# A transformer trunk layer: x loaded by features, W_ada packed for whole rows and cut into eleven groups, and the second runs of partial sums added last

## The chip, the cores and the metric

The kernel runs on one core of one Trainium2 chip. The metric is device time in microseconds (us), the median over runs of the kernel before; a single execution is also recorded by the hardware profiler, and all rows below come from that one. Engines: PE is TensorE (matmuls), DVE is VectorE, ACT is ScalarE, POOL is GpSimd, SP issues most transfers.

## The reference, cut to what matters

There are 512 tokens and 2048 features. One layer computes, in float32:

```python
mod = silu(c) @ W_ada + b_ada           # shift_a, scale_a, gate_a, shift_f, scale_f, gate_f
h = rms_norm(x) * (1 + scale_a) + shift_a
proj = h @ w_in                          # q/k/v, indexer q/k, latents, gates
y = W_o(sigmoid(g_a) * (o_A @ W_pA) + sigmoid(g_b) * (o_B @ W_pB))
x = x + gate_a * y
h = rms_norm(x) * (1 + scale_f) + shift_f
x = x + gate_f * (W_down(silu(conv(h W_up)_gate) * conv(h W_up)_value))
```

`o_A` is an attention over the keys that a top-k of indexer scores selects, `o_B` a dense causal attention. Only the part from `x` to a first share of the columns of `proj` is touched by the change.

## The kernel before

The 2048 features are 16 tiles of 128 (called tile 0 to 15). Each float32 factor is split into a high part `hi`, rounded by ACT, and a low part `lo`, the remainder, taken by DVE; a product is then three matmuls (hi·hi, hi·lo, lo·hi). For activations the split is L423 (ACT, hi) and L424 (DVE, lo), for weights L133 (ACT) and L134 (DVE).

**The first projection stage** computes the indexer's columns (name A, 1104 columns) and the keys, values and some gate columns (name B, 512 + 384 = 896 columns). Its unit is an *item*: one feature tile times one of the two column blocks, so A0 to A15 and B0 to B15, 32 items. An item is 21 matmuls of 128x512 (`quarter_k`) into seven of the eight PSUM banks. `PLAN` is a table that sets the order of items: all A items that follow one another without a B between them are one *run*, accumulated in the banks; as the last item of a run ends, `fin` stores the run's seven sums (`part`), or adds them to those of an earlier run on DVE (L376).

**The modulation** has to be there before an item: tile k of `h` needs scale and shift of tile k, which are 2 x 128 columns of `silu(c) @ W_ada`. Before, the 16 tiles are eight *groups* of two. For a group, 16 pieces of W_ada (one per 128 rows of the sum, each 128 rows x 2 x 256 columns, so two runs of 1 KB to a row) are loaded by SP (L328); DVE multiplies each by its entry of `silu(c)` and adds it up over the pieces (L339, L341; five of group 0's pieces go over PE instead, L333); PE sums over the partitions with a vector of ones (`ada_sum`, L347); DVE makes the columns (`ada_cols`, L312 and L354); and ACT applies scale and shift (L422) and rounds (L423).

**The start** loads x by tokens (4 x 4 tiles of 128x512), takes the squares with row sums on ACT (L268) and DVE (L266), the inverse root on POOL, scales rows (L274, L276), and turns x by 64 PE transposes of 128x128 (L297) with 16 copies by ACT (L301). Until the first item is ready, `keep_warm` (L254) puts small matmuls on PE.

**The order of the work.** Each engine has its own queue and takes it strictly in turn. The order in each queue is not the order of the source: a planner plays the program through with its own costs and decides; `tc.issue_after` and `tc.high_priority` bend it. Weights pass through five raw buffers and three pairs of hi/lo buffers, so that an item's split waits until the matmuls of the item three before it have ended. After the stage come the rotary tables (DVE), a transpose of the positions, further projections, and the indexer's scores (L598, L602), and much later the long stages of the FFN.

## Time and profile before

| | |
|---|---|
| time of the kernel, three runs | 2651.3, 2648.29, 2647.92 us; median 2648.29 us |
| span of the profiled execution | 2648.6 us, 0.3 us above the median |
| first matmul of the first projection stage | 37.95 us |
| end of its last matmul | 216.8 us |
| PE busy, whole span | 98% |

PE is busy nearly all of the time, so what the change can move lies in the first 8 per cent of the span. How to read a row: a group row has line, engine, operation, output<-input, shape and count, then busy time and mean ns of one, then the idle time of the engine just before these instructions and what ended it. A timeline row has start, duration and the instructions taken together, and in brackets the wait ahead of them with its releaser. A windows row has the stretch and its length, then the busy time of each engine, the clock that PE was granted (1.00 is full), and the share and rate of the transfers.

### The profile page before, as it was taken

Reading aid. Unit: us, or ns where it says so; the run is one execution under the profiler, and the core shown is the slowest. Engines: PE = TensorE matmul, PEld = TensorE weight load, DVE = VectorE, ACT = ScalarE, POOL = GpSimd, SP = SyncE. Lnnn points to the kernel's source line nnn. Section 1 sums busy time; section 2 is a strip of 40 time slices with the busy share of each in tenths; the row PEclk is TensorE's granted clock in tenths of the full one; section 3 lists DMA queues with packets and bytes.
Section 4 is the critical chain, followed back from the end, with each engine's and each line's share of the span. In section 5 each row is a group of like instructions: output and inputs, shape, how many; then the busy total and the mean of one; then the engine's idle time right before and its main releaser. Section 6 shows DMA issues by size and latency. Waiting matters only on the chain. (4 is left out here: it accounts for less than half of the span.)

```text
span 2648.6 us, 45089 instructions
## 1 busy us (share of the span) xinstructions
PE 2593.5 (98%) x17268; PEld 2349.6 (89%) x17268; DVE 2176.9 (82%) x3486; ACT 1249.7 (47%) x1951; POOL 366.0 (14%) x671
## 2 busy tenths in 40 slices
PE   8999999999999999999999999999999998999999
PEld 7777687779998777888789999999999998999999
DVE  7987975788878786975669899899899998878787
ACT  5333434344435544322545555555555556556454
POOL 1000011010022223200100000000000033314120
PEclk9999999999999999999999999999999999999999
DMA  9953135755675589974324433434434456767563
GB/s 342 344 163 100 36 100 188 228 155 169 198 243 178 156 273 352 301 254 137 135 74 145 145 115 130 144 116 130 145 124 140 148 173 190 206 163 214 141 198 114
DMA packets 215661, 464.32 MB, mean 175 GB/s; under 512 B 23786, under 2 KB 65156, under 8 KB 215444
## 3 DMA queue, kind: packets, MB, share of 16 engines
q1 hardware_dynamic: 170260, 344.93, 40.4%
q0 software_dynamic: 45152, 116.50, 14.9%
q8 instruction: 135, 2.21, 0.3%
q14 instruction: 82, 0.67, 0.1%
q10 hardware_dynamic: 32, 0.01, 0.0%
HBM read 397.11 MB, written 64.23 MB: 174 GB/s over the span
## 5 line engine op out<-in xcount | busy, mean ns | idle before, releaser
L1108 PE MATMUL bank<-slot,whl 128*128 128x256 f32 x3920 | 1103.0, 282 | 17.6 <-ACT slot L1008 5.9
L1109 PE MATMUL bank<-slot,whl 128*128 128x256 f32 x3920 | 1097.6, 281 | 0.7 <-DVE slot L142 0.7
L1110 PE MATMUL bank<-slot,whl 128*128 128x256 f32 x3920 | 1088.4, 282 | 6.1 <-DVE whl L142 6.1
L141 ACT ACTIVATE whl<-raw 128x1024 fp32r<-128x1024 f32 (+2 forms) x560 | 532.2, 953 | 632.6 <-PE bank L1109 408.7
L1108 PEld LDWEIGHTS bank<-slot,whl 128*128 128x128 f32 x3920 | 738.8, 189 | 24.5 <-ACT whl L141 7.9
L1109 PEld LDWEIGHTS bank<-slot,whl 128*128 128x128 f32 x3920 | 740.9, 189 | 1.1 <-DVE slot L142 0.9
L1110 PEld LDWEIGHTS bank<-slot,whl 128*128 128x128 f32 x3920 | 732.4, 188 | 7.2 <-DVE whl L142 7.1
L142 DVE TENSOR_TENSOR whl<-raw,whl 128x1024 fp32r<-128x1024 f32 (+2 forms) x560 | 605.6, 1087 | 131.9 <-ACT whl L141 123.7
L133 ACT ACTIVATE whl<-raw 128x1024 fp32r<-128x1024 f32 (+4 forms) x182 | 187.3, 1031 | 374.1 <-PE bank L147 184.3
L1004 DVE TENSOR_TENSOR raw<-raw 128x1024 f32<-128x1024 f32 (+2 forms) x320 | 347.4, 1086 | 4.9 <-DMA raw<-in_w_ups 1.4
L134 DVE TENSOR_TENSOR whl<-raw,whl 128x1024 fp32r<-128x1024 f32 (+4 forms) x182 | 215.8, 1186 | 154.7 <-ACT whl L133 148.3
L145 PE MATMUL bank<-whl,slot 128*128 128x512 f32 (+2 forms) x768 | 294.0, 395 | 9.3 <-ACT slot L423 6.1
L146 PE MATMUL bank<-whl,slot 128*128 128x512 f32 (+2 forms) x768 | 298.5, 389 | 0.4 <-DVE whl L134 0.4
L147 PE MATMUL bank<-whl,slot 128*128 128x512 f32 (+2 forms) x768 | 291.7, 385 | 0.0
L145 PE MATMUL bank<-slot,whl 128*128 128x512 f32 (+1 forms) x656 | 264.0, 406 | 6.1 <-DVE slot L733 3.8
L146 PE MATMUL bank<-slot,whl 128*128 128x512 f32 (+1 forms) x656 | 266.5, 407 | 1.9 <-DVE slot L741 1.9
L147 PE MATMUL bank<-slot,whl 128*128 128x512 f32 (+1 forms) x656 | 257.8, 401 | 0.1
L778 DVE SCALAR_TENSOR_TENSOR slot<-slot,c_act,slot 128x512 f32<-128x512 f32 x203 | 150.8, 748 | 45.4 <-DMA slot<-in_w_ada 43.5
L145 PEld LDWEIGHTS bank<-whl,slot 128*128 128x128 f32 x768 | 146.6, 192 | 41.7 <-ACT slot L423 6.8
L146 PEld LDWEIGHTS bank<-whl,slot 128*128 128x128 f32 x768 | 146.2, 190 | 30.2 <-issue 1.7
L147 PEld LDWEIGHTS bank<-whl,slot 128*128 128x128 f32 x768 | 144.7, 189 | 29.3 <-issue 0.7
L145 PEld LDWEIGHTS bank<-slot,whl 128*128 128x128 f32 (+1 forms) x656 | 123.8, 189 | 37.1 <-DVE slot L733 4.2
(292 smaller groups left out, 2722.2 us busy)
## 6 DMA issues: line engine op xcount, KB each, us to landing
slot<-in_w_ada SPq DMA_DIRECT2D x344, 256.0 KB, 5.3
raw<-in_w_ups SPq DMA_DIRECT2D x160, 512.0 KB, 3.6
raw<-in_w_in SPq DMA_DIRECT2D x50, 512.0 KB, 3.5
raw<-in_w_down SPq DMA_DIRECT2D x64, 384.0 KB, 4.8
raw<-in_w_down SPq DMA_DIRECT2D x64, 320.0 KB, 4.2
slot<-f POOLq DMA_DIRECT2D x154, 128.0 KB, 4.1
f<-slot POOLq DMA_DIRECT2D x66, 256.0 KB, 5.3
raw<-in_w_gs SPq DMA_DIRECT2D x32, 512.0 KB, 4.4
```

The lines of the kernel that those rows point to most:

```text
L133: A.activation(hi, raw[:, :w], AF.Copy)
L134: V.tensor_tensor(lo, raw[:, :w], r32(hi), ALU.subtract)
L141: A.activation(dst_hi, src, AF.Copy)
L142: V.tensor_tensor(dst_lo, src, r32(dst_hi), ALU.subtract)
L145: PE.matmul(o, lh, rh, start=first, stop=False)
L146: PE.matmul(o, lh, rl, start=False, stop=False)
L147: PE.matmul(o, ll, rh, start=False, stop=last)
L778: V.scalar_tensor_tensor(acc, ts[i], c_act[:, k:k + 1], acc, op0=ALU.mult, op1=ALU.add)
L1004: V.tensor_tensor(o[:, :W], a[:, :W], b[:, :W], op)
L1108: PE.matmul(o, wh[:, ks], rh, start=first and k == 0, stop=False, skip_group_check=True)
L1109: PE.matmul(o, wh[:, ks], rl, start=False, stop=False, skip_group_check=True)
L1110: PE.matmul(o, wl[:, ks], rh, start=False, stop=last, skip_group_check=True)
```

## The change

1. **x by features.** The host hands over x transposed as well, and L208 loads 16 tiles of 128 features x 512 tokens. ACT squares each (L271), DVE adds the squares (15 adds, L273), four small matmuls with ones sum over the partitions (L275), POOL takes the inverse root, PE spreads it over all partitions (L286) and DVE copies it out (L288, the tile `rbc`). Transposes and their copies are gone. Each tile of x is multiplied by `rbc` on DVE (`normed`, L302), two groups ahead of its use.
2. **W_ada packed.** The host packs the columns of shift and scale (`w_first`) so that each 128x512 piece has one run of 2 KB to a row (L329). A piece of a one-tile group holds two k pieces.
3. **Eleven groups**, `GROUPS`: tiles 0, 1, 2, 3 alone, then five pairs, then 14 and 15 alone. The first product of a group is ACT's (L348), others DVE's (L350, 256 or 512 wide), and some go over PE (L361): eight of group 0's, one of each of groups 4 to 8, two of the last two. A group's products are issued behind the columns (L374) of the group before it.
4. **The sum's place.** `SUM_IN` names the item inside which a group's sum stands in the source: B0 A1 A2 B3 B5 A7 A9 B11 A13 A14 for groups 1 to 10. It is the item, or the item but one, ahead of the first that needs the group.
5. **Order of items**: A0 B0 B1 A1 A2 A3 B2 to B7 A4 to A11 B8 to B13 A12 to A15 B14 B15.
6. **Runs.** The first and the second run of A and of B are stored by ACT (L416) in tiles of their own; third and, for B, fourth runs are added on DVE (L414) to the first. The fourteen adds of second into first (L396) are issued behind the last tile of h.
7. The keep-warm counts change to 42, 10 and 8, small constants on POOL move behind the inverse root, weights of four items are requested ahead, and the transpose of the positions (L521, L522) is issued behind the last tile of h.

The core of the diff, with what is only renamed left out:

```diff
+GROUPS = ((0, 1), (1, 1), (2, 1), (3, 1), (4, 2), (6, 2), (8, 2), (10, 2), (12, 2), (14, 1), (15, 1))
...
-    PLAN="A0 A1|A2 A3|B0 B1 B2 B3|A4 A5 A6 A7|B4 B5 B6 B7|A8 A9 A10 A11|B8 B9 B10 B11|A12 A13 A14 A15 B12 B13 B14 B15",
+    PLAN="A0 B0|B1 A1|A2|A3 B2 B3|B4 B5|B6 B7 A4 A5 A6 A7|A8 A9|A10 A11 B8 B9 B10 B11|B12 B13 A12 A13|A14|A15 B14 B15",
...
-    PEU=((2, 5, 8, 11, 14),) + ((),) * 7,
-    WU=(50, 20),
+    PEU=((0, 1, 4, 5, 8, 9, 12, 13),) + ((),) * 3 + ((15,),) * 5 + ((7, 15),) * 2,
+    SUM_IN='B0 A1 A2 B3 B5 A7 A9 B11 A13 A14',
+    WU=(42, 10, 8),
...
+        xs = [get() for _ in range(KD)]
+        for k in range(KD):
+            SP.dma_start(xs[k], xT_in[k * P:(k + 1) * P, :])
...
+    for k in range(KD):
+        t = sqx[(k - 1) % 5 + 1] if k else ssq
+        last_a = A.activation(t, xT[k], AF.Square)
+        if k:
+            V.tensor_tensor(ssq, ssq, t, ALU.add)
...
+    rbc = bcast_rows(rstd, bank[4])
+    last_h = [last_copy[0], last_a, last_copy[0]]
+
+    def normed(ks):
         for k in ks:
-            t = get()
-            A.activation(t, bank[k % 7], AF.Copy)
-            xT.append(t)
+            last_h[2] = V.tensor_tensor(xT[k], xT[k], rbc, ALU.mult)
...
+    def ada_mults(g):
         acc = accs[g % 2]
+        k0, n = GROUPS[g]
+        w = 2 * n * P
+        with tc.issue_after(last_h[2].ins):
...
+                    elif g not in begun:
+                        begun.add(g)
+                        with tc.issue_after(last_h[1].ins):
+                            A.activation(o, raw, AF.Copy, scale=c_act[:, k:k + 1])
+                    else:
+                        V.scalar_tensor_tensor(o, raw, c_act[:, k:k + 1], o, op0=ALU.mult, op1=ALU.add)
...
+    def next_tiles(g):
+        if g:
+            with tc.issue_after(mm_last[0].ins):
+                ada_sum(g)
+            mod_tiles(g)
+            if g + 2 < NG_A:
+                with tc.issue_after(last_h[2].ins):
+                    normed(range(GROUPS[g + 2][0], sum(GROUPS[g + 2])))
+            if g + 1 < NG_A:
+                ada_mults(g + 1)
             else:
...
+                        with tc.issue_after(last_h[0].ins):
+                            V.tensor_tensor(t[0:r], t[0:r], u[0:r], ALU.add)
+                        put(u)
...
+                t = part[name, min(runs[name], 3) % 3 or 1][i][0:r]
+                if runs[name] > 2:
                     V.tensor_tensor(t, t, b, ALU.add)
-                elif i % 2:
-                    V.tensor_copy(t, b)
                 else:
-                    A.activation(t, b, AF.Copy)
+                    last_h[1] = A.activation(t, b, AF.Copy)
...
-    V.tensor_copy(pos_f, posi)
+    with tc.issue_after(last_h[0].ins):
+        V.tensor_copy(pos_f, posi)
```

How the instructions stand in the queues shows at three places. **PE, a group's sum.** First PE's queue before, at the third sum, that of tiles 4 and 5, which item A4 is the first to need. `bank_73` is the bank of the modulation sums, `slot_351` the accumulated products; `slot_453` and `slot_454` are hi and lo of tile 1, `slot_516` the hi of tile 2.

```order
L147 MATMUL bank_70<-slot_453,whl 128x512
L147 MATMUL bank_71<-slot_453,whl 128x512
L147 MATMUL bank_72<-slot_453,whl 128x512
L347 MATMUL bank_73<-ones,slot_351 128x1 x4
L145 MATMUL bank_66<-whl,slot_516 128x512
L145 MATMUL bank_67<-whl,slot_516 128x512
L145 MATMUL bank_68<-whl,slot_516 128x512
```

Behind that sum stand B2 and B3, two items on tiles made long before. Now PE's queue of the changed kernel, at the sum of group 1 (tile 1): `slot_327` and `slot_328` are hi and lo of tile 0, `slot_445` the hi of tile 1.

```order
L155 MATMUL bank_71<-slot_327,whl 128x512
L153 MATMUL bank_72<-slot_327,whl 128x512
L154 MATMUL bank_72<-slot_328,whl 128x512
L155 MATMUL bank_72<-slot_327,whl 128x512
L361 MATMUL bank_73<-ones,slot_251 128x1 x2
L153 MATMUL bank_66<-whl,slot_445 128x512
L154 MATMUL bank_66<-whl,slot_445 128x512
L153 MATMUL bank_67<-whl,slot_445 128x512
```

Directly behind the sum stand the matmuls of item B1 on tile 1, whose hi is made from that very sum. The sums stand so, directly ahead of the item that needs them, at B0|B1, A1|A2, A2|A3, B3|B4, B5|B6, A9|A10, A13|A14 and A14|A15; inside A7 and B11 nine matmuls still follow the sum.

**DVE, the end of the stage.** First DVE's queue before, from the last lo of h (L424) on; `bank_66` and so on are the sums of the last run of A, `pos_c` the positions.

```order
L424 TENSOR_TENSOR slot_1350<-slot_354,slot_1349 128x512
L134 TENSOR_TENSOR whl<-raw,whl 128x1104 x2
L134 TENSOR_TENSOR whl<-raw,whl 128x896 x2
L376 TENSOR_TENSOR slot_406<-slot_406,bank_66 128x512
L376 TENSOR_TENSOR slot_409<-slot_409,bank_67 128x512
```

Then the changed kernel's DVE queue at the end of the adds of second runs; eleven more of them stand ahead of the first row, directly behind the last lo of h (L471).

```order
L396 TENSOR_TENSOR slot_519<-slot_519,slot_259 128x512
L396 TENSOR_TENSOR slot_524<-slot_524,slot_263 128x512
L396 TENSOR_TENSOR slot_529<-slot_529,slot_270 128x512
L136 TENSOR_TENSOR whl<-raw,whl 128x896 x2
L521 CAST slot_130<-slot_130 4x128
L414 TENSOR_TENSOR slot_393<-slot_393,bank_66 128x512
L414 TENSOR_TENSOR slot_398<-slot_398,bank_67 128x512
```

Between the last lo of h and the splits of the last two weights (L136, for B14 and B15) all fourteen adds of second runs have been put; the transpose of the positions (L522), which reads what L521 makes, stands on PE between A15 and B14.

**DVE, the first group.** The changed kernel's DVE queue from the copy of `rbc` (L288) to the first columns: the split of A0's weights (L136) stands ahead of the products of group 0, accumulated in `slot_250`.

```order
L288 COPY slot_241<-bank_70 128x512
L302 TENSOR_TENSOR slot_89<-slot_89,slot_241 128x512
L136 TENSOR_TENSOR whl<-raw,whl 128x1104
L350 SCALAR_TENSOR_TENSOR slot_250<-slot_255,c_act,slot_250 128x256
L350 SCALAR_TENSOR_TENSOR slot_250<-slot_259,c_act,slot_250 128x256 x2
L350 SCALAR_TENSOR_TENSOR slot_250<-slot_263,c_act,slot_250 128x256 x2
L350 SCALAR_TENSOR_TENSOR slot_250<-slot_270,c_act,slot_250 128x256 x2
L310 TENSOR_TENSOR mod<-bank_73,col_132 128x1 x2
L374 SCALAR_TENSOR_TENSOR s_a<-mod,col_132 128x1
```

DVE has seven products of 256 columns there, behind the split and ahead of the columns.

## The prediction

> **What bounds the kernel now.** The page comes first: who is busy over the span.

> ```profile
> span 2648.6 us, 45089 instructions
> PE 2593.5 (98%) x17268; PEld 2349.6 (89%) x17268; DVE 2176.9 (82%) x3486; ACT 1249.7 (47%) x1951; POOL 366.0 (14%) x671
> ```

> PE bounds the whole, so the change is worth what it does to PE's waits, work and clock in the first projection stage. Second, PE's timeline there.

> ```profile
> 37.95 0.50 PE L145 MATMUL bank<-whl,slot 128*128 128x512 f32 x1 [2.20 <-ACT slot L423]
> 51.50 1.05 PE L347 MATMUL bank<-ones,slot 128*128 128x1 f32 x8 [1.97 <-DVE slot L341]
> 55.20 0.80 PE L145 MATMUL bank<-whl,slot 128*128 128x512 f32 x1 [2.65 <-ACT slot L423]
> 107.21 2.93 PE L145 MATMUL bank<-whl,slot 128*128 128x512 f32 x6 [2.16 <-ACT whl L133]
> 146.12 0.50 PE L145 MATMUL bank<-whl,slot 128*128 128x512 f32 x1 [1.24 <-ACT slot L423]
> 194.20 0.40 PE L145 MATMUL bank<-whl,slot 128*128 128x512 f32 x1
> 196.75 0.39 PE L147 MATMUL bank<-slot,whl 128*80 128x512 f32 x1
> 216.81 0.44 PE L559 MATMUL bank<-ident,slot 80*128 80x80 f32 x4
> ```

> The first item starts at 37.95, the stage ends at 216.81. From 194.20 to 196.75 lie eleven steps, 0.232 us each, so 672 matmuls (32 items of 21) need 155.8 us. Third, two groups of 0 to 200 us and the granted clock by stretches.

> ```profile
> L145 PE MATMUL bank<-whl,slot 128*128 128x512 f32 x148 | 55.7, 426 | 9.3 <-ACT slot L423 6.1 <-ACT whl L133 2.9 <-ACT slot L380 0.3
> L347 PE MATMUL bank<-ones,slot 128*128 128x1 f32 x64 | 7.7, 241 | 2.0 <-DVE slot L341 2.0
> 38.00:60.00 22.00, 17.38 (x63) 13.40 (x64) 19.77 (x30) 5.12 (x7) 0.00 (x0) 0.77 1.09 358
> 100.00:120.00 20.00, 17.84 (x75) 13.94 (x74) 19.73 (x31) 3.98 (x4) 0.00 (x0) 0.91 1.05 353
> 120.00:140.00 20.00, 20.00 (x92) 16.33 (x91) 18.43 (x29) 6.79 (x8) 0.00 (x0) 1.00 1.07 369
> 160.00:180.00 20.00, 20.00 (x95) 16.39 (x94) 16.89 (x30) 9.36 (x12) 0.00 (x0) 1.00 0.32 97
> ```

> PE's waits in the stage are 9.3 - 2.2 + 2.0 = 9.1 us. The clock means 0.77 over 22 us and 0.91 over 20 are 10.1 and 3.6 us at half clock; some 3 us of these lie inside the waits at 51 to 55 us, so 10.7 us of work ran at half speed and lost 5.3. The sums of groups 1 to 7 take 56/64 of 7.7 = 6.7. Then 37.95 + 155.8 + 6.7 + 9.1 + 5.3 = 214.9, 1.9 short of 216.8; I carry this miss over. DVE is busy 19.8 of 22 and 19.7 of 20 us at first, 16.9 of 20 later: nearly full, but PE waits little for it, as the sums stand well ahead of their use.

> **The start.** Rows on arrival and on durations:

> ```profile
> 15.91 0.63 ACT L268 ACTIVATE slot<-slot 128x512 f32<-128x512 f32 x1
> 24.59 1.54 DVE L341 SCALAR_TENSOR_TENSOR slot<-slot,c_act,slot 128x512 f32<-128x512 f32 x2 [0.45 <-DMA slot<-in_w_ada]
> 11.00:14.00 3.00, 3.00 (x29) 3.00 (x28) 1.86 (x7) 2.90 (x9) 1.49 (x4) 1.00 1.05 401
> 15.00:20.00 5.00, 4.35 (x39) 4.08 (x39) 4.97 (x13) 2.75 (x7) 2.58 (x29) 1.00 1.10 352
> L133 ACT ACTIVATE whl<-raw 128x1104 fp32r<-128x1104 f32 x16 | 18.0, 1123 | 45.4 <-DMA raw<-in_w_in 30.1 <-PE bank L146 12.8 <-DVE s_a L354 2.5
> L134 DVE TENSOR_TENSOR whl<-raw,whl 128x1104 fp32r<-128x1104 f32 x16 | 20.9, 1304 | 10.9 <-ACT whl L133 10.9
> L602 DVE SCALAR_TENSOR_TENSOR slot<-slot,wi,slot 128x256 f32<-128x256 f32 x15 | 7.3, 484 | 5.1 <-ACT slot L598 4.0
> ```

> x has landed at 15.9 in either layout: both have 2 KB rows, which move at 401 GB/s (second-last window), against 352 for the 1 KB rows of W_ada. Behind x stand six packed pieces of 262 KB, 0.65 us each at 401: with the 1.2 us by which 24.59, the tenth piece of before, lies above ten steps of 0.745 from 15.9, they land at 21.0; A0's weights (565 KB, 1.4 us) at 22.4; the last two pieces at 23.7. ACT's hi of the weights takes 1.12 (to 23.6), DVE's lo 1.30 (to 24.9), and only then come DVE's seven products of 256 columns. The nearest row, L602 of that shape, has 484 ns, of which about 0.08 overlap in a row: 0.40 each, 27.7. The sum takes 0.25, columns and h 2.0 (below): **first item at 30.0** (28.7 if the split comes late, 31 if pieces come at 352 GB/s), 8.0 us earlier. The squares (16 on ACT, 15 adds on DVE) keep pace with x landing, and the root and its spread end ahead of 23 us, under the weights' transfer; the removed transposes lay under transfers too, so they give nothing by themselves. POOL's constants, moved behind the root, come long ahead of their use.

> **Transfers.** A feature tile needs 2.1 MB of W_ada and 1.02 MB of weights, 8.9 us at 352 GB/s and 7.8 at 401, and PE takes 9.7 for its two items. So the transfers keep their lead: group 1's eight pieces and B0's weights (459 KB) land by 31, and its sum is due at 40. Weights asked for earlier on SP's queue cost nothing under that lead; without it, a piece late costs PE 0.65. [...]

> **The boundaries.** What a sum costs when h is needed at once is shown at 51 to 55 us:

> ```profile
> 52.59 0.23 DVE L312 TENSOR_TENSOR mod<-bank,col 128x2 f32<-128x2 f32 x2 [1.15 <-PE bank L347]
> 52.85 0.16 DVE L354 SCALAR_TENSOR_TENSOR s_a<-mod,col 128x2 f32<-128x2 f32 x1
> 53.10 1.52 ACT L422 ACTIVATE slot<-slot,mod,s_a 128x512 f32<-128x512 f32 x2 [3.67 <-DVE s_a L354]
> 54.53 0.61 ACT L423 ACTIVATE slot<-slot 128x512 fp32r<-128x512 f32 x1
> ```

> Sum end at 52.55, columns, two scalings, one rounding, PE again at 55.20: 2.65 us for a pair. A single tile saves one scaling (1.52 for two), so about 2.0. In the changed PE queue the sum stands directly ahead of the item that needs it five times with a single tile (10.0) and three times with a pair (8.0); twice, in A7 and B11, nine matmuls (2.1) cover all but 0.55 (1.1). Sum **19.1**, whatever DVE does.

> DVE comes late besides. Products may start only behind the columns of the group before, so the short groups have little time:

> ```profile
> 59.83 4.72 DVE L341 SCALAR_TENSOR_TENSOR slot<-slot,c_act,slot 128x512 f32<-128x512 f32 x7
> 193.63 4.26 DVE L376 TENSOR_TENSOR slot<-slot,bank 128x512 f32<-128x512 f32 x7
> L134 DVE TENSOR_TENSOR whl<-raw,whl 128x896 fp32r<-128x896 f32 x15 | 16.3, 1085 | 5.2 <-ACT whl L133 5.2
> ```

> A product of 512 is 0.674 (4.72/7), an add or multiplication 0.61 (4.26/7), a split about 1.22 or 1.0 in a row. For A9|A10: two multiplications by `rbc` 1.2, waiting for hi 1.0, two lo 1.2, 14 products 9.4, two splits 2.4, the columns 0.5: 15.7; PE has nine matmuls, 0.55 and two items (9.7), 12.3. Late by 3.4. So counted, A2|A3 is late by 2.3, B5|B6 by 1.3, A14|A15 by 1.1: **8.1** (5.0 to 10.5). The products that go over PE are 28 behind group 0; at 0.24 each 6.7, of which 12 (2.9) stand where PE waits for DVE anyway: 3.8. The sums themselves are 30 x 0.24 = 7.0.

> **The end.** Behind A15's hi DVE has one lo (0.6), 14 adds (8.4; 13 of 128 rows, shape and engine of L376), two splits (2.0), the cast (0.2) and one more 0.6 until L522 and B14's lo let PE on: 11.8, against A15's 4.9 and 0.8 of PE's own: PE waits **6.1** (5.3 to 6.9). Before, nothing stood there. The stores of runs moved to ACT cost nothing, since ACT has over half its time free (9.4 of 20 us); the adds left to DVE there (L414) have room.

> **The clock.** Waits of 2.16 (107.21), 2.20 (37.95) and 1.97 + 2.65 (51.50, 55.20) were each followed by half clock, 1.24 (146.12) was not. A lowering lasts some 3.4 us (10.1 + 3.6 over four such) and loses up to 1.7. Of the nine long waits I take five, **8.0** (0 to 15.3).

> **The sum.** 30.0 + 155.8 + 10.8 + 19.1 + 8.1 + 6.1 + 8.0 + 1.9 = 239.8 for 216.8: +23.0. Behind the stage the queues are the same, so this reaches the end. 2648.6 + 23.0 - 0.3 (profiled span above the median) = 2671.3. With the low ends (28.7, late 5.0, tail 5.3, no half clock) it is 226.6, 2658; with the high ones (31, 10.5, 6.9, 15.3) 251.3, 2683.

> **The rivals.** *Faster.* Against before, 8.0 us are gained at the start and 9.1 + 5.3 of waits and clock could go; 3.8 + 0.3 of work on PE comes. So if all waits, lateness, tail and clock after the start cost under 18.3, the change is faster. It decides at the sums: were DVE ahead enough and the nine matmuls, or more, behind each sum, ten boundaries at 0.55 would be 5.5, and with the tail hidden the stage would end at 30.0 + 155.8 + 10.8 + 5.5 + 1.9 = 204, 2635. For it: DVE's total is about that of before (78 us of products either way) with more free time late. Against it: the queue puts eight sums last, 19.1 alone. With half the tail (3.0) and one lowering (1.7) left it is 208.7, **2640**, which I take. Chance 0.14.

> *The clock holds.* If PE waits of 2.0 to 2.65 us lower no clock and only the tail's 6.1 does (1.7), the sum is 239.8 - 6.3 = 233.5, **2665**. For it: each wait here stands alone, with 4.9 or 9.7 us of full work between, where 1.97 and 2.65 came together. Against it: 2.16 at 107.21 stood alone and was followed by half clock. Chance 0.12. [...]

> *Absorbed behind.* The scoring stage waits for DVE:

> ```profile
> 298.00:302.00 4.00, 2.33 (x7) 1.36 (x8) 4.00 (x13) 1.36 (x3) 0.00 (x0) 0.95 0.00 0
> 302.00:306.00 4.00, 3.81 (x9) 2.07 (x8) 4.00 (x11) 2.27 (x5) 0.00 (x0) 0.50 0.00 2
> 306.00:310.00 4.00, 4.00 (x10) 2.80 (x9) 4.00 (x13) 1.64 (x4) 0.32 (x1) 0.50 0.00 0
> ```

> PE idles 1.7 + 0.2 in the first two of these stretches and runs at half clock over some 10 us. If DVE's work there is not delayed with PE, up to 7 us come back (1.9 of waits and half of 10): **2664**. Against it: DVE is full throughout. Chance 0.08.

> *No change*: waits, lateness, tail and clock together near the 18.3 of the balance, 2648; chance 0.06.

> **How the numbers follow.** My forecast has 0.60; 2671. A difference of 0.2%, 5.3 us, is about what a measurement of this kernel can tell from none. Slower are the forecast, the held clock and the absorbed delay, 0.80; same 0.06; faster 0.14. The forecast's own range is 2658 to 2683. The whole range leaves out the fast half of the faster case and little above: 2643 to 2682.

> **What would show it.** In the changed profile: L153's first at 30; PE waits of 2.0 or 2.65 ahead of L153 at eight boundaries, behind L361; a wait of about 6 ahead of L522 or B14, with L396 on DVE meanwhile; a clock below 1.00 in several stretches of 30 to 235 us; the stage's end (L607) near 240. A stage that ends ahead of 217 proves me wrong, and PE waits under 1 us behind the sums say at which step.

## The result, and the profile after

The changed kernel takes **2685.78 us** (median of four runs, 2684.23 to 2686.99) against 2648.31 of the kernel before: ratio 1.0144, 95% interval 1.0129 to 1.0158. It is slower by 37.5 us, where 23.0 were forecast, with a time of 2682 as the high end. The first stage ends 41.9 us later (258.66 for 216.81), and 6.4 of these come back behind it: the spans differ by 35.4. (An execution's time lies 1.8 us above its span, 2685.8 for 2684.0 in the profiled one, so the profiled one of before ran some 2 us above the median; that is the rest to 37.5.) One execution further down, the profiled one of fill2, took 5896 us, more than twice any other, and is left out of its median.

The page of the changed kernel, first the same two lines as of before.

```profile
span 2684.0 us, 45152 instructions
PE 2607.9 (97%) x17280; PEld 2360.0 (88%) x17280; DVE 2192.4 (82%) x3519; ACT 1253.2 (47%) x1954; POOL 364.1 (14%) x668
```

PE is busy for 14.4 us more with 12 matmuls more; the table below puts most of that down to the clock. The other 21 us are waits. PE's timeline, one row for each kind of wait (wait and releaser in brackets):

```profile
24.95 1.58 PE L286 MATMUL bank<-ident,rstd 128*128 128x128 f32 x8
32.78 0.96 PE L361 MATMUL bank<-ones,slot 128*128 128x1 f32 x4 [1.79 <-DVE slot L350]
33.61 4.61 PE L261 MATMUL bank<-ones_r 128*128 128x128 f32 x20
37.87 0.77 PE L153 MATMUL bank<-whl,slot 128*128 128x512 f32 x1
...
51.06 0.51 PE L153 MATMUL bank<-whl,slot 128*128 128x512 f32 x1 [2.02 <-ACT slot L470]
...
162.52 1.85 PE L361 MATMUL bank<-ones,slot 128*128 128x1 f32 x8 [3.53 <-DVE slot L350]
166.96 0.80 PE L153 MATMUL bank<-whl,slot 128*128 128x512 f32 x1 [2.58 <-ACT slot L470]
...
246.65 0.22 PE L522 MATMUL bank<-ident,slot 4*128 4x4 f32 x1 [3.55 <-DVE slot L521]
...
258.66 0.44 PE L607 MATMUL bank<-ident,slot 80*128 80x80 f32 x4
```

The first item starts at 37.87, where before had 37.95: nothing was gained at the start. Behind a sum (L361) that stands directly ahead of its item PE waits 2.02 us for a single tile's h, 2.58 for a pair's (1.18 at the last, 0.40 where nine matmuls follow). PE's waits, grouped, over 35 to 262 us (total, times, longest):

```profile
PE bank L153 <- ACT slot L470: 17.8, 10, 2.6
PE bank L361 <- DVE slot L350: 8.3, 5, 3.5
PE bank L522 <- DVE slot L521: 3.6, 1, 3.6
PE bank L153 <- DVE slot L414: 0.5, 1, 0.5
```

And stretches of the stage (the third number from the end is the granted clock):

```profile
60.00:80.00 20.00, 13.80 (x44) 10.16 (x43) 17.32 (x35) 5.76 (x8) 0.00 (x0) 0.76 0.87 318
100.00:120.00 20.00, 15.81 (x68) 12.63 (x67) 17.51 (x27) 5.03 (x7) 0.00 (x0) 0.89 0.80 267
...
160.00:180.00 20.00, 14.89 (x53) 11.94 (x54) 15.80 (x25) 6.76 (x9) 0.00 (x0) 0.74 0.68 228
...
220.00:240.00 20.00, 15.46 (x61) 11.94 (x60) 13.99 (x30) 5.98 (x8) 0.00 (x0) 0.77 0.09 27
```

The trace shows a granted clock of 1.00 or 0.50 and nothing between, so a mean clock of 0.76 over 20 us is 9.6 us at half clock. All stretches from 38 to 260 us give 42.6 us so. In 4.8 us of these PE idles, and the other 38.0, counted at half the pace as in the forecast, cost it 19.0. (By the steps of its matmuls of 512 columns, 0.427 us at half clock for 0.232 at full, it would be 17.3, and the rest in the table 1.7 more.)

The stage, term by term, in the terms of the prediction:

| term | forecast | measured | |
|---|---|---|---|
| first item | 30.0 | 37.9 | +7.9 |
| 672 matmuls | 155.8 | 155.8 | |
| sums and products on PE | 10.8 | 13.2 | +2.4 |
| waits: boundaries, DVE late, end | 33.3 | 30.5 | -2.8 |
| half clock | 8.0 | 19.0 | +11.0 |
| rest | 1.9 | 2.3 | +0.4 |
| end of the stage | 239.8 | 258.7 | +18.9 |

(The sums and products are 116 small matmuls, 0.114 us from one to the next at full clock.)

### The profile page after: what moved, and what is told of

Same layout as the page of the kernel before. It is cut to its first block, busy times and chain, and to the rows that moved or that the text cites. A ratio compares the mean times of both kernels' runs of the same rounds, so it can differ in the third digit from the quotient of the medians.

```text
span 2684.0 us, 45152 instructions
## 1 busy us (share of the span) xinstructions
PE 2607.9 (97%) x17280; PEld 2360.0 (88%) x17280; DVE 2192.4 (82%) x3519; ACT 1253.2 (47%) x1954; POOL 364.1 (14%) x668
## 3 DMA queue, kind: packets, MB, share of 16 engines
q0 software_dynamic: 45152, 116.50, 14.5%
## 5 line engine op out<-in xcount | busy, mean ns | idle before, releaser
L147 ACT ACTIVATE whl<-raw 128x1024 fp32r<-128x1024 f32 (+2 forms) x560 | 532.2, 953 | 628.2 <-PE bank L1157 424.2
L136 DVE TENSOR_TENSOR whl<-raw,whl 128x1024 fp32r<-128x1024 f32 (+4 forms) x182 | 215.9, 1187 | 137.4 <-ACT whl L135 135.0
L153 PE MATMUL bank<-whl,slot 128*128 128x512 f32 (+2 forms) x768 | 301.7, 402 | 19.1 <-ACT slot L470 17.8
L154 PE MATMUL bank<-whl,slot 128*128 128x512 f32 (+2 forms) x768 | 303.9, 396 | 0.0
L155 PE MATMUL bank<-whl,slot 128*128 128x512 f32 (+2 forms) x768 | 290.0, 388 | 0.0
L153 PE MATMUL bank<-slot,whl 128*128 128x512 f32 (+1 forms) x656 | 262.8, 407 | 7.3 <-DVE slot L781 5.0
L153 PEld LDWEIGHTS bank<-whl,slot 128*128 128x128 f32 x768 | 149.7, 195 | 51.8 <-ACT slot L470 19.5
L154 PEld LDWEIGHTS bank<-whl,slot 128*128 128x128 f32 x768 | 150.2, 196 | 30.6 <-issue 0.7
L155 PEld LDWEIGHTS bank<-whl,slot 128*128 128x128 f32 x768 | 145.3, 189 | 30.2 <-issue 1.3
L153 PEld LDWEIGHTS bank<-slot,whl 128*128 128x128 f32 (+1 forms) x656 | 124.1, 189 | 38.5 <-DVE slot L781 5.4
```

The lines of the kernel that those rows point to most:

```text
L136: V.tensor_tensor(lo, raw[:, :w], r32(hi), ALU.subtract)
L147: A.activation(dst_hi, src, AF.Copy)
L153: PE.matmul(o, lh, rh, start=first, stop=False)
L154: PE.matmul(o, lh, rl, start=False, stop=False)
L155: mm_last[0] = PE.matmul(o, ll, rh, start=False, stop=last)
```

## The experiments

Four questions were open: what makes the first item late, whether the waits or the half clock behind them cost the most, what makes DVE late, and what part of the change would be worth keeping. The theory was that the terms add up, so that each one taken away gives its size back; the rival, that DVE's products (or, with these cheaper, the chain from a sum to h) set the pace, so that what is taken from one wait appears in another. Each ratio is to the kernel before on the same chip (medians 2645.7 to 2648.2). "Stage end" is the start of what follows the last of the 672 matmuls. In the changed kernel that is L607, the first transpose behind the stage. In tail and in the four combos PE goes on to the next projection first (21 of its matmuls in tail), and the transpose comes later. In tail the first row is the stage's end, the second the transpose:

```profile
251.23 0.40 PE L155 MATMUL bank<-whl,slot 128*128 128x512 f32 x1
256.12 0.37 PE L610 MATMUL bank<-ident,slot 80*128 80x80 f32 x3
```

All this is read from one profiled execution of each. The first item moves in these even where the edit doesn't touch the start: 37.87 in the changed kernel, 35.16 to 37.95 in tail, fill, fill2_again and hide. So the time from the first item to the stage's end stands beside it:

| run | first item | stage end | from one to the other |
|---|---|---|---|
| before | 37.95 | 216.81 | 178.9 |
| changed | 37.87 | 258.66 | 220.8 |
| start | 32.21 | 256.51 | 224.3 |
| tail | 35.16 | 251.23 | 216.1 |
| fill | 36.12 | 268.00 | 231.9 |
| fill2_again | 35.96 | 254.75 | 218.8 |
| acc2 | 34.44 | 247.63 | 213.2 |
| hide | 37.95 | 256.04 | 218.1 |
| combo | 34.99 | 241.32 | 206.3 |
| combo_plan | 33.69 | 240.87 | 207.2 |
| combo_hide | 33.68 | 232.40 | 198.7 |
| combo_fill | 33.59 | 241.14 | 207.6 |

**start.** The spread of the root (L286) is put ahead of group 0's products on PE, and eight keep-warm matmuls fill the wait for the root (`mv5` is the matmul of L275, `mv4` that of the spread).

```diff
     keep_warm(WU[2])
+    with tc.issue_after(mv5.ins):
+        keep_warm(8)
...
-    ada_sum(0)
+    with tc.issue_after(mv4[0].ins):
+        ada_sum(0)
```

> The changed kernel with one thing in another order: the four matmuls that spread the inverse root over the partitions (ahead of the copy of rbc) stand on PE ahead of the group 0 products that go over PE, and eight keep-warm matmuls bridge the root. In the changed kernel the spread waited on PE behind three such products with half-clock keep-warm matmuls, from 21.7 to 24.95 us, the copy of rbc began at 26.57 and the first item at 37.87. Theory A (that queue is what delays the first item): copy of rbc at about 23.4, first item at 33 to 34.5, the stage's end 258.7 less 3 to 5, the time 2681 to 2683. Rival B (DVE's products of group 1 and their transfers set the pace anyway): the first item earlier by 3 to 5, but the stage's end by under 1.5, the time 2684 to 2686.

2683.64 us, 1.0134 (1.0112 to 1.0155). DVE's queue in this kernel, against the changed kernel's behind it:

```profile
22.66 0.69 DVE L291 COPY slot<-bank 128x512 f32<-128x512 f32 x1 [0.59 <-PE bank L289]
```

```profile
26.57 0.69 DVE L288 COPY slot<-bank 128x512 f32<-128x512 f32 x1 [5.44 <-PE bank L286]
27.29 0.69 DVE L302 TENSOR_TENSOR slot<-slot,slot 128x512 f32<-128x512 f32 x1
27.90 1.30 DVE L136 TENSOR_TENSOR whl<-raw,whl 128x1104 fp32r<-128x1104 f32 x1
29.12 3.61 DVE L350 SCALAR_TENSOR_TENSOR slot<-slot,c_act,slot 128x256 f32<-128x256 f32 x7
```

The copy comes 3.9 us earlier, the keep-warm matmuls run at full clock (2.48 us for 4.61), and the first item starts at 32.21, 5.7 earlier. Not all of it is the edit's: the sum of squares over the partitions (L275), which it doesn't touch, comes 0.9 earlier here (18.43 for 19.37). So some 3.0 us are the spread's place, behind three products of group 0 and their keep-warm matmuls, and 2.1 the clock in the later ones. The stage ends only 2.15 us earlier (256.51), between the two expectations: the waits for DVE's products grow from 8.3 to 10.8, that at the end from 3.6 to 4.1, and the half clock takes 1.1 more. Most of what the start gains is given back behind it, to DVE first of all.

**tail.** The fourteen adds of second runs are issued behind the last split.

```diff
-                        with tc.issue_after(last_h[0].ins):
-                            V.tensor_tensor(t[0:r], t[0:r], u[0:r], ALU.add)
...
+            with tc.issue_after(last_split[0].ins):
+                V.tensor_tensor(t[0:r], t[0:r], u[0:r], ALU.add)
```

> The changed kernel with the fourteen adds of second runs behind the splits of the last two weights instead of ahead of them. Theory A (the adds hold up the cast and the splits): the waits of 3.55 us ahead of the transpose of the positions and 0.47 ahead of B14 go, and the half clock behind them (1.7): the stage's end 258.7 less 4 to 6, 253 to 255, and the time 2680 to 2682. Rival B (the adds only move on): the sums of A and B are then late for what reads them behind the stage, PE waits there instead, and the time stays at 2684 to 2686.

2685.57 us, 1.0139 (1.0123 to 1.0156). Both waits at the end are gone and the stage ends 7.4 us earlier (251.23); 2.7 of these are its earlier first item. In the other 4.7 stand the two waits (4.0) and 2.2 less half clock, against 1.4 more of waits for products. The end lies ahead of the 253 to 255 that theory A expected, but the time stays where its rival had it. In the medians 0.2 us is left, and an interval of some 4 us to either side can't tell 4.7 from nothing. What the scoring stage does meanwhile shows in one stretch of this kernel, of the changed one, and of before:

```profile
300.00:345.00 45.00, 42.60 (x188) 29.32 (x186) 40.67 (x114) 21.38 (x45) 2.31 (x2) 0.85 0.04 12
```

```profile
300.00:345.00 45.00, 42.59 (x210) 30.49 (x209) 41.47 (x118) 21.18 (x40) 3.29 (x3) 0.98 0.11 36
```

```profile
300.00:345.00 45.00, 44.12 (x180) 33.24 (x181) 43.85 (x102) 19.89 (x30) 1.01 (x1) 0.89 0.19 52
```

PE idles 2.4 us here and in the changed kernel, but runs at half clock for 13.5 us here, for 1.8 there, for 9.9 before; with what follows just behind the stretch, up to 352 us, it is 20.5, 6.8 and 10.2. That the edit's fourteen adds, now on DVE behind the stage, cause the difference is not shown; but the clock behind the first stage moves by several us with what comes ahead of it.

**fill, fill2, fill2_again.** Dummy matmuls stand where PE waits at the boundaries, to see whether the clock then holds. In the first they stand directly behind and ahead of the sums.

```diff
+    PRE = {2: 2, 3: 6, 5: 6, 7: 14, 10: 4}
+    POST = {1: 7, 2: 7, 3: 7, 4: 9, 5: 9, 7: 9, 9: 7, 10: 3}
+    def filler(n):
+        for _ in range(n):
+            PE.matmul(bank[7][:, 384:512], r32(ones_r), r32(ones_r), ...)
```

> The changed kernel with small dummy matmuls (their output is never read) on PE in the waits of the stage: some behind each sum that stands directly ahead of its item, some ahead of the five sums for which DVE is late. They do not shorten a wait, they only keep PE busy in it. In the changed kernel 20 us of PE time were lost to half clock in the stage, in nine stretches. Theory A (the lost clock adds to the waits one to one): no half clock between 42 and 235 us, and the stage's end earlier by 15 to 18, 241 to 244, the time 2668 to 2671. Rival B (DVE sets the pace where a sum is late, so the half clock ahead of such a sum is covered by the wait): half clock gone all the same, but the waits for DVE's products grow from 8.3 to 13 to 17 us, the stage's end earlier by 5 to 9 only, 250 to 254, the time 2677 to 2681. Rival C (the clock falls only after a full idle window and not after waits of 2 to 2.6 us): little changes in the clock column and in the time.

2703.0 us, 1.0206 (1.0189 to 1.0223); stage end 268.00, which none of the three expected. The edit itself added a wait. Its PE queue at the first sum:

```profile
46.58 0.61 PE L373 MATMUL bank<-ones,slot 128*128 128x1 f32 x4 [0.45 <-DVE slot L350]
47.05 1.81 PE L359 MATMUL bank<-ones_r 128*128 128x128 f32 x14
50.87 0.50 PE L153 MATMUL bank<-whl,slot 128*128 128x512 f32 x1 [2.02 <-ACT slot L485]
```

The columns read the bank into which the dummies write, and so waited for these: 2.02 us of wait stand behind 1.8 of dummies. Half clock falls from 42.8 to 27.3 us, but with the longer waits the price of the clock can't be read from it. fill2 puts the dummies behind the reading of the columns (counts 6 and 8 for 7 and 9).

```diff
             mod_tiles(g)
+            if g in POST:
+                with tc.issue_after(last_mv[0].ins):
+                    filler(POST[g])
```

> The dummy matmuls again, but those behind a sum now stand behind the reading of that sum's columns: in the run before, DVE's columns waited for the dummies too, since both go to the same PSUM bank, so each chain became 1.6 to 3 us longer instead of being filled. Now PE idles about 0.8 us until the columns are read and is busy in the rest of the wait. The measure is the stage's end (258.7 in the changed kernel), since the queues behind the stage can come out in another order. Theory A (lost clock adds to the waits one to one): half clock falls from 41 to under 10 us between 42 and 260, the end to 241 to 245. Rival B (where a sum is late, DVE sets the pace and the lost clock ahead of it is covered): half clock falls as much, waits for products grow by 5 to 9 us, the end only to 250 to 254. Rival C (waits of 2 to 2.6 do not lower the clock): half clock stays near 40 us.

2691.6 us (median of four), 1.0169 (1.0152 to 1.0186). fill2_again is the same kernel with a profile.

> The run with dummies behind the columns once more, for a profile: the profiled execution of the last one ran more than twice as long as every other (5896 us, all engines), so only its times count (2690 to 2697 us). What is to be seen is how a stage with its waits filled comes out. Theory A (lost clock adds to the waits one to one): half clock under 10 us between 42 and 260, the end at 241 to 245. Rival B (where a sum is late DVE sets the pace): little half clock, the waits for products or the dummies in their place longer by 5 to 9 us, the end at 250 to 256. After the times, 2690 and more, A is already unlikely.

2689.83 us in that one execution. Its waits and two of its stretches:

```profile
PE bank L374 <- DVE slot L352: 7.3, 5, 3.0
PE bank L539 <- DVE slot L538: 4.9, 1, 4.9
```

```profile
60.00:80.00 20.00, 16.25 (x81) 13.16 (x81) 17.86 (x35) 6.65 (x10) 0.00 (x0) 0.91 0.80 287
160.00:180.00 20.00, 19.25 (x93) 15.31 (x94) 17.52 (x27) 6.95 (x9) 0.00 (x0) 1.00 0.59 190
```

The clock holds much better, 0.91 and 1.00 for 0.76 and 0.74; half clock after 42 us falls from 41 to 20.5 us, which frees about 9 us of PE. But the stage ends only 3.9 earlier (254.75), and 1.9 of that is the first item: dummies ahead of the late sums take some 7.5 us, and PE still waits 7.3 there, 14.8 for 8.3 before. So most of what the faster clock saves turns into waiting for DVE, as the rival had it. The half clock is real, but its 19.0 us can't be added to the lateness as if each stood alone.

**acc2.** A group's products go in turn into two accumulators, and the sum takes both.

```diff
+                        odd[0] += 1
+                        o2 = accs2[g % 2][:, :w]
+                        if odd[0] == 1:
+                            V.tensor_scalar(o2, raw, c_act[:, k:k + 1], None, op0=ALU.mult)
+                        else:
+                            o = o2 if odd[0] % 2 else o
+                            V.scalar_tensor_tensor(o, raw, c_act[:, k:k + 1], o, ...)
...
-            todo.append((accs[g % 2], ones))
+            todo += [(accs2[g % 2], ones), (accs[g % 2], ones)]
```

> The changed kernel with two accumulators to a group in place of one: DVE's products go to them in turn, and PE's sum takes both (18 to 20 more small matmul instructions of 0.24 us). Before, products of two groups alternated between two accumulators in long stretches and took 0.66 us apart; in the changed kernel each adds to the tile that the one just ahead of it wrote, and they stand 0.787 us apart (512 columns) and 0.52 (256). Theory A (a product that adds to what the one just ahead of it wrote waits for that one's end): 0.66 and 0.40 apart, DVE is ready 1.5 us earlier at each group, the waits ahead of the five late sums fall from 8.3 to 3 to 4 us, and the stage ends 4 to 8 us earlier, the time 2678 to 2682. Rival B (the distance is that of the packed pieces, whichever tile they add to): 0.787 and 0.52 stay, and the extra sums make the stage 2 to 4 us longer, the time 2686 to 2690.

2684.55 us, 1.0132 (1.0114 to 1.0151), but the stage ends **11.0 us earlier**, at 247.63, more than theory A expected (4 to 8), while the time misses its 2678 to 2682; 3.4 of these come ahead of the first item, where the keep-warm matmuls run at full clock (2.1) as they do in tail. DVE's products in the changed kernel, and in this one:

```profile
101.79 9.41 DVE L350 SCALAR_TENSOR_TENSOR slot<-slot,c_act,slot 128x512 f32<-128x512 f32 x12
```

```profile
94.61 6.30 DVE L359 SCALAR_TENSOR_TENSOR slot<-slot,c_act,slot 128x512 f32<-128x512 f32 x9
```

0.78 us each (9.41/12) where each adds to the tile that the one just ahead wrote, 0.70 (6.30/9) where they go to two tiles in turn for the most part. Before had 0.674 in the row that the prediction used: products of two groups stood there in turn. Its trace has the other price too, with ten products of one group in a row, 0.78 each (7.83/10):

```profile
41.02 7.83 DVE L341 SCALAR_TENSOR_TENSOR slot<-slot,c_act,slot 128x512 f32<-128x512 f32 x10
```

PE's waits in acc2:

```profile
PE bank L153 <- ACT slot L479: 11.5, 6, 2.6
PE bank L531 <- DVE slot L530: 3.6, 1, 3.6
...
PE bank L370 <- DVE slot L359: 0.3, 1, 0.3
```

Those for products fall from 8.3 to 0.3, those for h from 17.8 to 11.5. Of the 11.0 us some 10 are gone at the end of the run (span 2683.3 for 2684.0). Taking the same matmul in both traces, 7.8 of them are left at 380 us, behind the scoring stage (half clock 13.7 us for 6.8), 4.7 at 592 and 0.3 at 880. Behind the first stage the planner's queues come out otherwise, and two waits stand there that the changed kernel has not, or shorter; 6.8 us of half clock follow the second:

```profile
531.96 0.49 PE L795 MATMUL bank<-slot,slot 128*128 128x128 f32 x2 [2.70 <-DVE slot L790]
...
809.09 0.58 PE L1167 MATMUL bank<-slot,whl 128*128 128x256 f32 x1 [4.92 <-DVE whl L148]
```

Before has a wait of 3.60 at that second place (its L1110, at 773.33), also with 6.8 us of half clock behind it, and the changed kernel 0.26 there and 1.59 a little later, with none: this is the largest part of the 6.4 us that come back behind the stage.

**hide.** The last nine matmuls of an item are issued behind a sum made inside it.

```diff
+        def behind():
+            return tc.issue_after(last_mv[0].ins) if due else nullcontext()
...
-            mm3(bank[6][0:80, :], wh[:, 1024:1104], wl[:, 1024:1104], hh, hl, first, last)
+            with behind():
+                mm3(bank[6][0:80, :], wh[:, 1024:1104], wl[:, 1024:1104], hh, hl, first, last)
```

> The changed kernel with one thing in another order: the last nine matmuls of an item (2.1 us) stand on PE behind the sum that is made inside it, at all ten sums, where the planner had moved eight sums behind them. Theory A (the sum's place makes the boundary's wait): the waits for h fall from 17.8 us to 3 to 5, where DVE is ready in time they are gained (B0|B1, B3|B4, A13|A14), where it is late the wait moves ahead of the sum; half clock falls from 41 us to 25 to 30: the stage's end from 258.7 to 246 to 251. Rival B (DVE's chain from columns over products to the next sum sets the pace at nearly every boundary): what PE gains behind the sums it waits ahead of them, the end at 254 to 258.

2683.09 us, 1.0137 (1.0122 to 1.0152); stage end 256.04, 2.6 earlier, as the rival expected. Its waits:

```profile
PE bank L362 <- DVE slot L351: 24.1, 6, 5.7
PE bank L530 <- DVE slot L529: 5.0, 1, 5.0
PE bank L153 <- ACT slot L478: 1.1, 3, 0.4
```

The waits for h are gone (1.1 for 17.8), and the waits for DVE's products have taken their place (24.1 for 8.3). Alone, this cures nothing.

**combo, combo_plan, combo_hide, combo_fill.** combo is start, acc2 and tail in one. combo_plan adds other places for items and sums, combo_hide the nine matmuls behind each sum, combo_fill the dummies of fill2 behind the sums.

```diff
-    PLAN="A0 B0|B1 A1|A2|A3 B2 B3|B4 B5|B6 B7 A4 A5 A6 A7|A8 A9|A10 A11 B8 B9 B10 B11|B12 B13 A12 A13|A14|A15 B14 B15",
+    PLAN="A0 B0|B1 A1|A2|A3 B2 B3|B4 B5 A4 A5|A6 A7 B6 B7|B8 B9 A8 A9|A10 A11|A12 A13 B10 B11 B12 B13|A14|A15 B14 B15",
-    SUM_IN='B0 A1 A2 B3 B5 A7 A9 B11 A13 A14',
+    SUM_IN='B0 A1 A2 B3 A5 A7 A9 A11 B11 A14',
```

> The changed kernel with three of the edits at once: the spread of the inverse root first, two accumulators to a group, the adds of second runs last. Singly they moved the stage's end by 2.2, 11.0 and 2.5 us, and the first item by 5.7 in the first. Theory A (DVE's chain of products was what took up the earlier start, and it no longer does): they add up or more, the end at 258.7 less 16 to 20, 239 to 243. Rival B (the waits for columns and h, ten boundaries of 2.0 to 2.6, now set the pace alone): the end at 244 to 248. The time: 2684 less as much as the queues behind the stage let through, 2665 to 2680 by A, 2675 to 2684 by B.

2680.12 us, 1.0124 (1.0101 to 1.0148); stage end 241.32, 17.3 earlier, as theory A expected (239 to 243). From the first item to the end it is 14.5 less, where the three alone come to 8.8 (3.5 more in start, 7.6 less in acc2, 4.7 less in tail): that cheaper products keep the earlier start from being given back would fit, but no run shows it by itself.

> The same three edits and another table of items: the A items of a pair of tiles stand behind its B items (A4 A5 behind B4 B5, A6 A7 ahead of B6 B7, A8 to A13, then B10 to B13, A14 A15, B14 B15), two runs more, and the sums of groups 5 to 9 stand one to three items earlier than in the changed kernel. So DVE can go on to the next group's products sooner, and pairs have two to four items of cover. Theory A (DVE idles while a sum that is ready waits for its late place, and comes late for the short groups behind it): the waits for products all but go behind group 4, and the end is 4 to 8 us ahead of the kernel with the three edits alone. Rival B (the boundaries' chains stay and two more runs cost 14 adds): no earlier end, or 1 to 3 us later.

2677.08 us, 1.0117 (1.0102 to 1.0132); stage end 240.87, hardly earlier than combo's. The waits for h shrink from 13.9 to 10.0, but one of 4.56 for weights (at 140.37) comes in their place.

> The three edits (spread first, two accumulators, adds last; end of the stage 246.2) and the nine matmuls behind each sum. With the accumulators DVE is ready in time at most sums. Theory A (now the sum's place is what is left): the waits for h fall from 14 to 3 to 5 us and half clock with them, the end at 230 to 236. Rival B (DVE still late): the end at 241 to 246.

2668.39 us, **1.0081** (1.0065 to 1.0097); stage end 232.40. The profiled executions lie below their medians here (2662.1) and in combo (2672.2). Theory A had its end at 230 to 236. The main waits of combo, then all of combo_hide:

```profile
PE bank L155 <- ACT slot L478: 13.9, 9, 2.6
PE bank L375 <- DVE slot L364: 2.4, 2, 1.9
```

```profile
PE bank L376 <- DVE slot L365: 8.2, 6, 4.0
```

With DVE's products cheaper, hiding the sums now pays: 8.9 us at the stage's end (241.32 to 232.40) and 11.7 in the medians, where hide alone had 2.6 at the stage's end. Boundaries and DVE's lateness are two chains, of which the longer is paid; only both together give the time back. What is left against before at the stage's end is 15.6 us, although the first item comes 4.3 earlier: 176 small matmuls on PE for 56 take 13.3 us more, the half clock 7.8 more (13.2 for 5.4).

> The three edits and the dummies behind the columns at eight boundaries, none ahead of a sum. DVE is ready in time at most sums now, so that here the price of the clock alone is to be seen. Theory A (a wait of 2.0 to 2.6 costs its clock besides, when DVE is not the pace): half clock falls from over 30 us to under 15, and the end comes 6 to 10 us earlier than 246.2. Rival B (lost clock is covered even here): the end stays at 244 to 247.

2676.28 us, 1.0112 (1.0095 to 1.0129); stage end 241.14. The half clock only falls from 30.7 to 27.3 us, where under 15 was expected: this leaves the price of the clock alone open.

**b_acc2, b_pack, b_xpack.** Parts of the change, or of its cure, on the kernel before: two accumulators for groups 0 to 2; the packed W_ada alone; the packed W_ada with x by features. The core of each, in this order:

```diff
+                    acc = accs2[g % 2] if g < 3 and n % 2 else accs[g % 2]
...
-            SP.dma_start(raw.rearrange("p (s n) -> p s n", s=2),
-                         w_ada[k * P:(k + 1) * P, 0:2 * D].rearrange("p (s n) -> p s n", s=2)
-                         [:, :, g * 256:(g + 1) * 256])
+            SP.dma_start(raw, w_first[g * KD + k])
...
+            SP.dma_start(xs[k], xT_in[k * P:(k + 1) * P, :])
...
+                V.tensor_tensor(xT[k], xT[k], rbc, ALU.mult)
```

> The kernel before with two accumulators for groups 0 to 2 and nothing else (12 small matmul instructions more, 2.9 us of PE, four of them ahead of the first item). There, too, the products of group 1 each add to the tile that the one just ahead wrote. Theory A (each then waits for the other's end, 0.12 us a product): group 1 is ready 1.5 to 2 us earlier, the wait of 1.97 us at 51.5 goes, with part of the half clock behind it: the stage ends 1 to 3 us earlier, the time 2644 to 2648. Rival B (transfers set group 1's pace): nothing earlier, the extra sums cost 2 us, 2649 to 2651.

2649.36 us, 1.0009 (0.9998 to 1.0020): no change. The wait of 1.97 us that the second accumulator was to remove is gone from its trace, and the waits for weights grow from 3.3 us to 4.7.

> The kernel before with W_ada packed by the host so that each piece has one run of 2 KB to a row in place of two of 1 KB, groups of two as before; the queues of all engines are those of before. Theory A (rows of 1 KB come at 352 GB/s and rows of 2 KB at 390 to 400, and transfers set the first item and some of DVE's early waits): pieces land sooner, the first item (37.95) 1 to 2 us earlier, the stage's end 1 to 4 earlier, the time 2642 to 2646. Rival B (transfers of W_ada are not what the path waits for): 2646 to 2648 as before.

2645.17 us, 0.9993 (0.9984 to 1.0002): no change that can be measured, though the transfers are faster and the stage of its profiled execution ends 3.3 us earlier (213.51), from a first item that comes no earlier (38.35). Its windows, for 352 and 358 GB/s before:

```profile
15.00:20.00 5.00, 3.09 (x28) 2.77 (x26) 5.00 (x17) 2.31 (x7) 0.71 (x1) 0.99 1.05 383
20.00:30.00 10.00, 9.65 (x76) 9.65 (x77) 7.85 (x15) 9.74 (x19) 0.75 (x1) 0.83 1.05 393
```

> The kernel before with W_ada packed and with x by features (squares on ACT and DVE, the root spread by PE, each tile of x multiplied by it on DVE, two groups ahead), but with its own eight groups, its own table of items and its own sums. Theory A (the loss lies in the eleven groups, their sums and DVE's chain, not in x's new way): the first item at 34 to 37, the stage's end at 214 to 222, the time 2643 to 2653, within 5 us of before. Rival B (DVE's 16 multiplications and 15 adds and the later root cost more than the transposes did): the first item no earlier than 37, the end at 224 or later, the time 2655 or more.

2654.71 us, 1.0034 (1.0021 to 1.0048); stage end 223.74, 6.9 later than before's. DVE and PE at its start:

```profile
25.77 6.11 DVE L292 TENSOR_TENSOR slot<-slot,slot 128x512 f32<-128x512 f32 x10
```

```profile
38.88 1.86 PE L334 MATMUL bank<-ones,slot 128*128 128x1 f32 x8 [8.62 <-DVE slot L328]
43.33 0.80 PE L145 MATMUL bank<-whl,slot 128*128 128x512 f32 x1 [2.59 <-ACT slot L411]
```

In before's order x by features costs 9 us: all sixteen multiplications by the root, ten of them in one row, stand on DVE ahead of the first sum, which comes at 38.88. So of these two parts the one brings nothing that can be measured and the other costs. That the larger part of the 37.5 us lies in groups, sums and their order follows by subtraction alone: no run has these without the two parts.

## Why the prediction was wrong

The direction and most of the mechanism held. Two terms were too small, the half clock by 11.0 us and the first item by 7.9; together they are the stage's whole miss of 18.9, and the others cancel.

1. *The boundaries*: 19.1 forecast, 17.8 measured; 2.02 for a single tile and 2.58 for a pair against 2.0 and 2.65, and 0.40 where nine matmuls follow against 0.55. Right but for A14|A15, where transposes (L514) fill part of the wait (1.18).
2. *DVE late*: 8.1 forecast, 8.3 measured in five places, the longest 3.53 for 3.4 forecast. The size is luck in part. The forecast let 2.9 us of products on PE pass inside this lateness; the measured waits begin behind those products, so like for like DVE was later by some 11. A product took 0.78 and not 0.674, which the prediction took from a row of two groups in turn: acc2, with 0.70, has 0.3 left.
3. *The end*: 6.1 forecast, 4.0 measured. DVE's part was sized well; the fourteen adds took 8.51 us for 8.4:

```profile
235.95 8.51 DVE L396 TENSOR_TENSOR slot<-slot,slot 128x512 f32<-128x512 f32 x14
```

   The wait was shorter because A15 ran at half clock (234.25 to 241.08) and took 7.7 us for 4.9: here the half clock stood under the wait, and the two terms did not add up.
4. *The clock* is the step that failed: "Of the nine long waits I take five, **8.0** (0 to 15.3)." Nine stretches of half clock came, four of them of two or three windows of 3.41 us (the first reaches back ahead of the first item), 42.6 us in all, and cost 19.0. The bound of 15.3 for nine lowerings of one window each was too low as well: behind the waits of 3.53 and 2.58 at 162 and 167 the clock stayed down for 10.2 us.
5. *The start* failed too: "the root and its spread end ahead of 23 us". The root did (21.7); the spread stood on PE behind three products of group 0, partly at half clock, so that the split of the first weights ended at 29.2 and not 24.9 (+4.3), some 3.0 of which start gives back. Products of 256 took 0.52 and not 0.40 (+0.7), the chain from sum to h 0.7 more, and the ten keep-warm matmuls ahead of the first item 2.1 more at half clock. Those 2.1 are chance: in tail, whose start is the same, they run at full clock.
6. *Behind the stage*: "Behind the stage the queues are the same, so this reaches the end" failed by 6.4 us, in the other direction. Taking the same matmul in both traces, the changed kernel lies 41.8 us behind at the stage's end, 39.9 behind the scoring stage (half clock 6.8 us there for 10.2), 38.2 at 793 and 35.8 at 881, past the wait of 3.60 that before has and the half clock that follows it. The rival that had the delay absorbed in the scoring stage was partly true (some 2 us there).
7. *The faster rival* hoped for sums with nine matmuls behind them and a hidden tail. combo_hide has just this, and takes 2668: with every wait but 8.2 us gone, the sums' own matmuls and the clock still cost more than there is to gain. No version here beat the kernel before by more than can be measured.

What stays open: the price of the half clock by itself. All three attempts to hold the clock brought work or waits of their own.

## What to carry to other kernels

A sum put directly ahead of its use costs the whole chain behind it (here 2.0 to 2.6 us in seven places), and the clock that falls in the wait can cost nearly as much again (a stretch of 3.41 us at half clock, counted at half the pace, is 1.7). In this kernel it fell at seven of the eight places with a wait of 2 us or more, and for three windows where two such waits followed one another. If two chains end near each other, the chain to h and DVE's products, easing one only shows the other: try both at once before giving up on either. Read a gain at the end of its stage and again at the end of the run: acc2 had 11.0 us in the one and about 1 in the other. And mark the end of a stage by its own last instruction: the planner may move what follows, as it did in tail.

## What the runs showed of the hardware

```profile
134.30:137.70 3.40, 3.40 (x28) 3.18 (x26) 0.00 (x0) 0.00 (x0) 0.00 (x0) 1.00 0.11 17
137.70:141.10 3.40, 3.40 (x12) 2.74 (x12) 2.55 (x7) 2.16 (x4) 0.00 (x0) 0.50 0.18 60
```

  The first holds 22 matmuls of 128x1, and the clock falls from 1.00 to 0.50 behind it without any wait. So this sum over the partitions by single columns was followed by half clock as the waits were.
- **A DVE product that adds to the tile just written came 0.12 us later.** Of products of 512 columns directly behind one another in before, the 18 that follow one on the same tile start 0.779 to 0.798 us behind it (median 0.787), the 44 that follow one on the other accumulator 0.660 to 0.666 (median 0.663). In the changed kernel all 49 follow one on the same tile, 0.778 to 0.789 us behind it.
